# Low parts of two gate blocks on GpSimd instead of VectorE, fewer filter taps there, and weight parts that begin at four different places in their slots

## The chip, the core and the metric

One NeuronCore of a Trainium2 chip runs the whole program. Its engines each work through a queue of their own, strictly in order, and wait for one another by semaphores. The profile's short names are used throughout: PE is TensorE (matrix products), PEld its loads of the stationary operand, DVE is VectorE, ACT is ScalarE, POOL is GpSimd, SP is SyncE, whose queue issues nearly all DMAs. The metric is the device time of one execution in microseconds (us). Before the change the median of three runs is 541.69 us (541.57 to 543.17). One further execution was profiled: 542.99 us, of which 540.7 us lie between its first and last instruction (the span).

## What is computed

One layer of a decoder block on 256 tokens of width 1,024, in float32. What matters here is the first third:

```python
h = rms_norm(x, norm_mix_g)
u, q, kc, vc, ks, vs, kw, vw, g_nsa, g_conv, g_attn = split(h @ w_in)
conv_out = conv_module(u)            # gated, 31-tap filter per channel, layer norm, silu, product
nsa_out  = nsa_attention(q, kc, vc, ks, vs, kw, vw, g_nsa)   # compressed + selected + window attention
y = sigmoid(g_conv) * conv_out + sigmoid(g_attn) * nsa_out
x = x + y @ w_out                    # then cross attention and a SwiGLU FFN
```

`ga0`..`ga3` are the four blocks of `g_attn` (256 channels each), `gc0`..`gc3` those of `g_conv`. The compressed branch first runs a small product over the keys' and values' blocks (`compress_blocks`: sum over 32 positions, then silu).

## The kernel before, in words

**Products in three parts.** PE's fast float32 form (`F32R`) keeps fewer bits, so every operand is held as a high part and a low part, and each product of a GEMM is made three times: high by high, high by low, low by high (`rows`, L234). A block of weights arrives in two halves of 128 partitions x 1,024 elements (512 KB). `raw` (L205) takes one of 4 slots of tag `w` and issues the DMA on SP; `split` (L173) makes the high part on ACT (`hi`, L177) and the low part `lo = w - hi` (L179), on POOL for the names in `aside` (L184: from `u1` to `ga1`) and on DVE for all others. High and low parts have 5 slots each (`whi`, `wlo`), 4,096 bytes long, so they all begin at the same place modulo 4,096. A slot of `w` is free, and the DMA that wants it can leave SP, when both parts of its former tenant are made.

**The filter.** 31 taps per channel, eight blocks of 128 channels, done in pairs. `taps_v` (L411) accumulates on DVE in PSUM (`yp`), one instruction per block and tap (L422). For the first pair, taps 0 to `FIRST_G`-1 = 17 go another way (`taps_g`, L425): ACT multiplies (`vw`, L431), POOL adds into `yt` (L434); DVE does taps 18 to 30 into `part01`, and POOL adds that at the end (L436). `convolve` hands a counted number of such steps to the engines between the GEMMs.

**Gates and first scores.** `gate(0)` and `gate(1)` (L665) multiply `ga0`, `ga1`; between the rows of `gate(1)` stand the compressed scores `cs_ps` (L695), which DVE adds into `nsc` (L698). `gt_ps` (L712) turns the heads' gate logits; ACT takes `sgt` from it (L715), and DVE makes `igc` and `igd` from `sgt` (L718). `scores(0)` (L722) needs two PSUM buffers `s1` (tag `s`, two buffers, one of them last held by `cs_ps`) and one `s0` (tag `s0`, a single buffer, last held by `gt_ps`). Then `between` (L813) goes on with `ga2`, `ga3`, `gc0`..`gc3`, `v0`..`v3`, cut into rows between the attention heads' work.

**What sets the order.** Each engine's queue is laid down when the program is built: a scheduler simulates the engines and takes instructions by priority. `behind(mark)` adds that an instruction comes after `mark` on the same engine. Nothing is reordered at run time: an instruction whose input is late holds up all behind it on its engine, and a DMA that waits on SP holds up all later DMAs.

**The compressed product.** `hidden` (L517) makes `z_ps` in 32 products with 64 columns of weights and 5 x 15 columns of keys or values (rows of 15 out of 16).

Of the kernel before, what the change touches and what calls it, by code (L numbers as in the profile page):

```python
# [10 lines left out]
F32R = mybir.dt.float32r  # L11
AF = mybir.ActivationFunctionType
ALU = mybir.AluOpType
AX = mybir.AxisListType

P = 128
D = 1024
S = 256
NB = D // P
HEADS = 16  # L20
GROUPS = 4
HD = 64
# [8 lines left out]
NCMP = 15  # L31
WARM = 8
LINE = 16
FIRST_G = 18

CHUNKS = (
    [f"k{j}" for j in range(1, 4)] + [f"u{j}" for j in range(8)]
    + ["kc", "vc"] + [f"q{j}" for j in range(4)] + ["ks", "kw", "vs", "vw"]
    + [f"ga{j}" for j in range(4)] + [f"gc{j}" for j in range(4)]
    + [f"pw{j}" for j in range(4)] + [f"wo{j}" for j in range(4)]  # L40
    + [f"xq{j}" for j in range(4)] + [f"v{j}" for j in range(4)]
    + [f"xo{j}" for j in range(4)] + [f"f{j}" for j in range(NF)]
)
CHUNK_AT = {n: i for i, n in enumerate(CHUNKS)}
# [53 lines left out]
def tile_hybrid_block(  # L98
# [49 lines left out]
    def aux(name, shape, tag, bufs):  # L148
        return axp.tile(shape, F32, tag=tag, name=name, bufs=bufs)

    def f(ap):
        return ap.bitcast(F32)
# [18 lines left out]


    def split(w, shape, name):  # L173
        hi = small(f"{name}h", shape, F32R, tag="whi", bufs=5)
        lo = small(f"{name}l", shape, F32R, tag="wlo", bufs=5)
        with behind(*first.get(name, ())):
            copy = nc.scalar.activation(hi, w, AF.Copy)  # L177
            eng = nc.gpsimd if name[:-2] in aside else nc.vector
            splits[name] = copy, eng.tensor_tensor(out=lo, in0=w, in1=f(hi[:]), op=ALU.subtract)  # L179
        return hi, lo  # L180


    first, splits = {}, {}
    aside = CHUNKS[CHUNK_AT["u1"]:CHUNK_AT["ga2"]]  # L184

    def behind(*marks):

# [167 lines left out]
    mem, h = (memh, meml), (hh, hl)  # L355
# [110 lines left out]
    with behind(loads["u6_1"]):  # L466
# [33 lines left out]
    kvt = [long(f"{n}t", slot, (P, 8, GROUPS + 1, 16)) for n, slot in (("k", 11), ("v", 13))]  # L500
    for kv, name in enumerate(("kc", "vc")):
        ps = gemm(name, h)
        kc = kvt[kv]
        for g in range(2):
            for odd in range(2):
                at = ps[HD * g:HD * g + HD].rearrange("p b (m l o) -> p b l m o", l=8, o=2)[:, :, :, :, odd]
# [10 lines left out]
    def hidden():  # L517


        z_ps = aux("z_ps", [P, GROUPS + 1, NCMP], "o", 1)  # L520
        with in_line():
            for l in range(16):
                for kv in range(2):
                    mm = nc.tensor.matmul(z_ps[HD * kv:HD * kv + HD], lhsT=w1t[:, kv, l],
                                          rhs=kvt[kv][:, l % 8, :, l // 8:l // 8 + NCMP], start=l == 0, stop=l == 15)
        last[:] = [mm]
        zs = small("zs", [P, GROUPS, NCMP], tag="zs", bufs=2)
        at = small("at", [P, 1])
        nc.scalar.activation(at, z_ps[:, GROUPS, 0:1], AF.Copy)
        sig = nc.scalar.activation(zs, z_ps[:, :GROUPS], AF.Sigmoid, bias=at)  # L530

        with behind(sig):
            nc.scalar.activation(small("exps", [P, 1]), eps1, AF.Exp)
        z1 = zz[:HD, 0, :64].rearrange("p (g n) -> p g n", g=GROUPS)[:, :, 0:NCMP]
        nc.vector.scalar_tensor_tensor(out=z1, in0=z_ps[:HD, :GROUPS], scalar=at[:HD], in1=zs[:HD], op0=ALU.add, op1=ALU.mult)
        nc.vector.scalar_tensor_tensor(out=zs[HD:], in0=z_ps[HD:, :GROUPS], scalar=at[HD:], in1=zs[HD:], op0=ALU.add, op1=ALU.mult)
        nc.scalar.activation(zz[HD:, 1].rearrange("p (g r n) -> p g r n", g=GROUPS, r=4)[:, :, :, 0:NCMP],
                             zs[HD:].unsqueeze(2).to_broadcast([HD, GROUPS, 4, NCMP]), AF.Copy)

# [17 lines left out]
    for j in range(4):  # L557
# [5 lines left out]
                                       op0=ALU.mult, op1=ALU.subtract)  # L563
        vec = nc.vector.scalar_tensor_tensor(out=q1[0:64], in0=ps[64:128], scalar=-0.125, in1=f(q1[64:128]),
                                             op0=ALU.mult, op1=ALU.subtract)
# [33 lines left out]
    with behind(loads["vw_0"]):  # L599
        nc.sync.dma_start(wg, wgn)  # L600

    wgs = small("wgs", [P, NB, 2, 64], F32R, tag="wlo", bufs=5)
    nc.scalar.activation(wgs[:, :, 0], wg, AF.Copy)
    nc.gpsimd.tensor_tensor(out=wgs[:, :, 1], in0=wg, in1=f(wgs[:, :, 0]), op=ALU.subtract)

# [109 lines left out]
    nc.scalar.activation(sgt, gt_ps, AF.Exp, scale=-1.0)  # L715
    for to, g in ((igc, sgt[:, :, 0:HEADS]), (igd.rearrange("p h t b -> p t b h"),
                                              sgt[:, :, HEADS:3 * HEADS].rearrange("p t (b h) -> p t b h", b=2))):
        nc.vector.tensor_scalar(out=to, in0=g, scalar1=2.0, scalar2=2.0, op0=ALU.mult, op1=ALU.add)  # L718


    def heads_of(hp):
# [2 lines left out]
    def scores(hp):  # L724

        g = hp // 2
        nbp = bias_of(hp)
        s0 = aux(f"s0_{hp}", [P, 2, 2, P], "s0", 1)
        p0 = small(f"p0_{hp}", [P, 2, 2, P], tag="p0", bufs=2)
        p1 = []  # L730
        for k, hd in enumerate(heads_of(hp)):
            s1 = aux(f"s1_{hd}", [P, 2, S], "s", 2)
            with in_line():
                for i, t in enumerate((kdh, kdl)):
                    nc.tensor.matmul(s1, lhsT=qh(hd, 1), rhs=t[:, g].rearrange("p b t -> p (b t)"), start=i == 0, stop=i == 1)  # L735
                for i, t in enumerate((kdh, kdl)):
                    mm = nc.tensor.matmul(s0[:, k], lhsT=qh(hd, 0), rhs=t[:, g, :, 0:P], start=i == 0, stop=i == 1)
            p1.append(small(f"p1_{hd}", [P, 2, S], tag="pr", bufs=4))
            for br in range(2):
                nc.vector.tensor_tensor_reduce(out=p1[k][:, br], in0=s1[:, br], in1=nbp[:, k], scale=1.0, scalar=3e38,  # L740
                                               op0=ALU.add, op1=ALU.min, accum_out=mins[:, hd, 1, br:br + 1])
        last[:] = [mm]
        for k, hd in enumerate(heads_of(hp)):
            for br in range(2):
                least = nc.vector.tensor_tensor_reduce(out=p0[:, k, br], in0=s0[:, k, br], in1=nbp[:, k, P:S], scale=1.0, scalar=3e38,
                                               op0=ALU.add, op1=ALU.min, accum_out=mins[:, hd, 0, br:br + 1])
        first["scores"] = least,
        return p0, p1
# [737 lines left out]
```

## Time and profile before

| what | us |
|---|---|
| median of three runs (541.57 to 543.17) | 541.69 |
| the profiled execution | 542.99 |
| its span | 540.7 |
| PE busy | 529.8 (98%) |
| DVE busy | 455.0 (84%) |
| ACT busy | 357.6 (66%) |
| POOL busy | 155.7 (29%) |

Matmuls are pipelined: each lasts longer than the distance to the next one, so PE counts as busy even where it is slowed. What PE loses shows in two other ways: in rows with an idle time before them, and in the distance between the starts of equal products. Engines other than PE matter where PE, or a DMA that PE's weights come from, waits for them. A timeline row merges equal instructions that follow each other; its columns are start, length, engine, line, operation, output<-inputs, shapes and count.

### The profile page before, as it was taken

The page shows a single profiled execution, that of the slowest core. Times are in us where ns is not written, and L with a number is a line of the kernel's source. Part 1 is how long each engine was busy: PE and PEld are TensorE (multiplying, and loading weights), DVE is VectorE, ACT ScalarE, POOL GpSimd, SP SyncE. Part 2 cuts the span into 40 slices and gives each one's busy share as a digit, 9 for nine tenths or more (in the row PEclk, how much of TensorE's full clock was granted, in tenths as well). Part 3 has the DMA queues.
Part 4 walks back from the last instruction along what each step waited for, and adds up shares of the span by engine and source line. Part 5 has one row for each costly group of instructions (what it writes and reads, how often), then busy time and mean ns, then how long its engine had stood idle before and what let it go on. Part 6 is the DMA issues. An engine that isn't in the chain of part 4 may idle for free.

```text
span 540.7 us, 10518 instructions
## 1 busy us (share of the span) xinstructions
PE 529.8 (98%) x3963; PEld 495.4 (92%) x3963; DVE 455.0 (84%) x913; ACT 357.6 (66%) x649; POOL 155.7 (29%) x109
## 2 busy tenths in 40 slices
PE   9999999999979999999999999999999999999995
PEld 8999999999969988999999999988888888888884
DVE  4868899899989898885869676588899999879996
ACT  4675475787674887969547755576676677648563
POOL 0079999899971000301003100150000000000001
PEclk9999999999979999999999999999999999999999
DMA  8927954665153744438655742757846668438632
GB/s 323 402 83 233 369 180 162 208 195 161 62 183 126 223 151 135 135 98 233 205 198 170 270 138 98 220 171 205 261 158 193 198 208 237 159 121 245 198 118 78
DMA packets 30739, 101.52 MB, mean 188 GB/s; under 512 B 3296, under 2 KB 5856, under 8 KB 30304
## 3 DMA queue, kind: packets, MB, share of 16 engines
q1 hardware_dynamic: 29104, 96.99, 53.8%
q0 software_dynamic: 864, 2.62, 2.8%
q10 hardware_dynamic: 720, 1.23, 0.6%
q8 instruction: 31, 0.51, 0.4%
q14 instruction: 20, 0.16, 0.1%
HBM read 99.59 MB, written 1.25 MB: 186 GB/s over the span
## 4 chain that ended last, share of the span: by engine, by line
PE 60%; DVE 1%; ACT 0%; issue 0%; ACTq 0%; DVEq 0%
PE ps_f L1203 15%; PE ps_f L1205 7%; PE fo L1242 6%; PE ps_xo L246 4%; PE ps_v L246 4%; PE ps_pw L246 4%; PE ps_wo L246 4%; PE ps_xq L246 4%; PE m L1242 4%; PE xo_ps L970 1%; PE xs L970 1%; PE o L801 1%; PE pt_a L780 1%; PE s L735 1%; PE o L798 1%; PE pt_b L780 0%
## 5 line engine op out<-in xcount | busy, mean ns | idle before, releaser
L422 DVE SCALAR_TENSOR_TENSOR yp<-vt,ppt,yp 128x256 f32<-128x256 f32 x196 | 78.4, 486 | 0.2
L1203 PE MATMUL ps_f<-g,f_1h 128*128 128x512 f32 x176 | 49.0, 397 | 0.0
L1203 PE MATMUL ps_f<-g,f_0h 128*128 128x512 f32 x176 | 48.3, 396 | 0.0
L1203 PEld LDWEIGHTS ps_f<-g,f_1h 128*128 128x128 f32 x176 | 32.9, 188 | 7.6
L1203 PEld LDWEIGHTS ps_f<-g,f_0h 128*128 128x128 f32 x176 | 29.9, 188 | 4.0
L179 DVE TENSOR_TENSOR f_1l<-f,f_1h 128x1024 fp32r<-128x1024 f32 x22 | 27.4, 1248 | 5.0 <-ACT f_1h L177 4.1
L1205 PEld LDWEIGHTS ps_f<-g,f_0l 128*128 128x128 f32 x176 | 26.8, 188 | 3.9
L179 DVE TENSOR_TENSOR f_0l<-f,f_0h 128x1024 fp32r<-128x1024 f32 x22 | 26.8, 1219 | 1.8 <-ACT f_0h L177 1.7
L177 ACT ACTIVATE f_1h<-f 128x1024 fp32r<-128x1024 f32 x22 | 23.2, 1056 | 7.0 <-PE ps_xo L246 3.7
L1205 PE MATMUL ps_f<-g,f_0l 128*128 128x256 f32 x176 | 27.4, 277 | 0.0
L179 POOL TENSOR_TENSOR u_0l<-u,u_0h 128x1024 fp32r<-128x1024 f32 x7 | 17.3, 2469 | 31.7 <-ACT u_0h L177 31.7
L434 POOL TENSOR_TENSOR yt<-yt,vw 128x512 f32<-128x512 f32 x17 | 25.2, 1482 | 3.0 <-ACT vw L431 2.7
L1205 PE MATMUL ps_f<-g,f_1l 128*128 128x256 f32 x176 | 25.8, 277 | 0.0
L177 ACT ACTIVATE f_0h<-f 128x1024 fp32r<-128x1024 f32 x22 | 23.1, 1050 | 2.7 <-DMA f<-in_wst_dram 1.3
L1206 ACT ACTIVATE ab<-ps_f 128x256 f32<-128x256 f32 x44 | 16.5, 375 | 11.6 <-PE ps_f L1205 10.9
L755 ACT ACTIVATE p<-p,mins 128x256 f32<-128x256 f32 x32 | 15.9, 503 | 10.3 <-DVE mins L740 10.3
L1205 PEld LDWEIGHTS ps_f<-g,f_1l 128*128 128x128 f32 x176 | 22.6, 188 | 0.0
L1119 POOL DMA_DIRECT2D spare<-in_wfo_dram x1 | 0.9, 866 | 74.2 <-DVE ab L1207 74.2
L1207 DVE TENSOR_TENSOR ab<-ps_f,ab 128x256 f32<-128x256 f32 x44 | 18.3, 419 | 3.0 <-ACT ab L1206 2.8
L290 ACT ACTIVATE uh<-sl 128x256 fp32r<-128x256 f32 x22 | 9.1, 414 | 14.0 <-DVE sl L1211 14.0
L179 POOL TENSOR_TENSOR u_1l<-u,u_1h 128x1024 fp32r<-128x1024 f32 x7 | 17.9, 2552 | 0.0
L310 POOL TENSOR_TENSOR nt_l<-nr_l 128x2 f32<-128x2 f32 x4 | 1.0, 241 | 55.0 <-DVE nr_l L307 54.7
(658 smaller groups left out, 1701.0 us busy)
## 6 DMA issues: line engine op xcount, KB each, us to landing
f<-in_wst_dram SPq DMA_DIRECT2D x44, 512.0 KB, 5.5
fo<-in_wfo_dram SPq DMA_DIRECT2D x16, 512.0 KB, 3.9
u<-in_wst_dram SPq DMA_DIRECT2D x14, 512.0 KB, 8.3
q<-in_wst_dram SPq DMA_DIRECT2D x8, 512.0 KB, 4.5
ga<-in_wst_dram SPq DMA_DIRECT2D x8, 512.0 KB, 4.1
gc<-in_wst_dram SPq DMA_DIRECT2D x8, 512.0 KB, 3.7
v<-in_wst_dram SPq DMA_DIRECT2D x8, 512.0 KB, 6.6
pw<-in_wst_dram SPq DMA_DIRECT2D x8, 512.0 KB, 5.8
```

The lines of the kernel that those rows point to most:

```text
L177: copy = nc.scalar.activation(hi, w, AF.Copy)
L179: splits[name] = copy, eng.tensor_tensor(out=lo, in0=w, in1=f(hi[:]), op=ALU.subtract)
L246: mm = nc.tensor.matmul(ps[:, b], lhsT=lhsT, rhs=rhs, start=row + b + kb == 0, stop=kb == NB - 1 and row == 2 and b == 1)
L422: nc.vector.scalar_tensor_tensor(out=out[:, i] if t == ts[-1] else acc[i], in0=v, scalar=w, in1=acc[i], op0=ALU.mult, op1=ALU.add)
L434: nc.gpsimd.tensor_tensor(out=yt[:, 0:2], in0=yt[:, 0:2], in1=pr, op=ALU.add)
L755: exp.append(nc.scalar.activation(p1[k][:, br], p1[k][:, br], AF.Exp, scale=-1.0, bias=mins[:, hd, 1, br:br + 1], accum_out=sums[:, hd, 1, ...
L970: mm = nc.tensor.matmul(o, lhsT=lhsT, rhs=rhs, start=n == 0, stop=n == len(order) - 1)
L1203: nc.tensor.matmul(ps, lhsT=hs[kb // 4][0][:, kb % 4, cs], rhs=fg[:, :, kb], start=kb == 0, stop=False)
L1205: nc.tensor.matmul(ps[:, 1], lhsT=hs[kb // 4][1][:, kb % 4, cs], rhs=fg[:, 0, kb], start=False, stop=kb == NB - 1)
L1206: nc.scalar.activation(ab[:, b], ps[:, 0], AF.Copy)
L1207: joins[b] = nc.vector.tensor_tensor(out=ab[:, b], in0=ps[:, 1], in1=ab[:, b], op=ALU.add)
L1242: mm = nc.tensor.matmul(o, lhsT=a[x], rhs=b[w], start=start and n == 0, stop=stop and n == 2)
```

## The change

1. `aside` ends at `gc0` instead of `ga2`: the low parts of `ga2` and `ga3` (four halves) are made by POOL instead of DVE.
2. `FIRST_G` is 14 instead of 18: four taps of the first pair go from ACT and POOL (8 multiplications, 4 additions) to DVE (8 instructions of L422).
3. `igc` and `igd` are made by ACT instead of DVE.
4. The halves of `gc0` are set behind the first scores (`first["gc0_0"]`), and after each of its low parts, made by DVE, POOL copies one element of it (`pause_...`), so that POOL's queue waits there for DVE.
5. The slots of high and low parts are 4,160 bytes long, and the parts begin 0, 16, 32 or 48 bytes into them, by turns.
6. `z_ps` takes 65 neighbouring columns instead of 5 x 15.

```diff
-FIRST_G = 18
+SLOT = 1024 + LINE
+FIRST_G = 14
...
     def split(w, shape, name):
-        hi = small(f"{name}h", shape, F32R, tag="whi", bufs=5)
-        lo = small(f"{name}l", shape, F32R, tag="wlo", bufs=5)
+        at = 4 * (len(splits) % 4)
+        hi, lo = (sb.tile([P, SLOT], F32R, tag=f"w{t}", name=f"{name}{t[0]}", bufs=5)[:, at:at + shape[1] * shape[2]].rearrange(
+            "p (k n) -> p k n", k=shape[1]) for t in ("hi", "lo"))
         with behind(*first.get(name, ())):
             copy = nc.scalar.activation(hi, w, AF.Copy)
             eng = nc.gpsimd if name[:-2] in aside else nc.vector
             splits[name] = copy, eng.tensor_tensor(out=lo, in0=w, in1=f(hi[:]), op=ALU.subtract)
+            if name[:-2] == "gc0":
+                nc.gpsimd.tensor_copy(small(f"pause_{name}", [P, 1], tag="exps"), f(lo[:])[:, 0, 0:1])
...
-    aside = CHUNKS[CHUNK_AT["u1"]:CHUNK_AT["ga2"]]
+    aside = CHUNKS[CHUNK_AT["u1"]:CHUNK_AT["gc0"]]
...
-        z_ps = aux("z_ps", [P, GROUPS + 1, NCMP], "o", 1)
+        z_ps = aux("z_ps", [P, 16 * GROUPS + 1], "o", 1)
...
-                                          rhs=kvt[kv][:, l % 8, :, l // 8:l // 8 + NCMP], start=l == 0, stop=l == 15)
+                                          rhs=kvt[kv][:, l % 8].rearrange("p g n -> p (g n)")[:, l // 8:l // 8 + 16 * GROUPS + 1],
+                                          start=l == 0, stop=l == 15)
...
-        nc.vector.tensor_scalar(out=to, in0=g, scalar1=2.0, scalar2=2.0, op0=ALU.mult, op1=ALU.add)
+        nc.scalar.activation(to, g, AF.Copy, scale=2.0, bias=2.0)
...
     p = [scores(0)]
+    first["gc0_0"] = first["scores"]
```

How the queues stand around the first scores. PE's order and the order of the weights' DMAs stay the same there. `ga2_0` is the first half of block `ga2`, an `h` or `l` at its end the high or low part; a last number is the buffer's.

POOL, from the end of `ga1`'s low parts to the sum for the layer norm, before:

```order
L179 TENSOR_TENSOR ga1_1l_2032<-ga1_1_2029,ga1_1h_2031 128x1024
L434 TENSOR_TENSOR yt_354<-yt_354,vw12_1862 128x512
L434 TENSOR_TENSOR yt_354<-yt_354,vw13_1866 128x512
L434 TENSOR_TENSOR yt_354<-yt_354,vw14_1870 128x512
L434 TENSOR_TENSOR yt_354<-yt_354,vw15_1874 128x512
L434 TENSOR_TENSOR yt_354<-yt_354,vw16_1878 128x512
L434 TENSOR_TENSOR yt_354<-yt_354,vw17_1882 128x512
L436 TENSOR_TENSOR yt_354<-yt_354,part01_355 128x512
L626 TENSOR_TENSOR ysum_1915<-yt_354 128x512
```

and with the change:

```order
L181 TENSOR_TENSOR ga1_1l_2024<-ga1_1_2021,ga1_1h_2023 128x1024
L438 TENSOR_TENSOR yt_354<-yt_354,vw12_1870 128x512
L181 TENSOR_TENSOR ga2_0l_2109<-ga2_0_2106,ga2_0h_2108 128x1024
L181 TENSOR_TENSOR ga2_1l_2180<-ga2_1_2177,ga2_1h_2179 128x1024
L181 TENSOR_TENSOR ga3_0l_2212<-ga3_0_2209,ga3_0h_2211 128x1024
L438 TENSOR_TENSOR yt_354<-yt_354,vw13_1874 128x512
L181 TENSOR_TENSOR ga3_1l_2242<-ga3_1_2239,ga3_1h_2241 128x1024
L440 TENSOR_TENSOR yt_354<-yt_354,part01_355 128x512
L183 COPY pause_gc0_0_2304<-gc0_0l_2301 128x1
L633 TENSOR_TENSOR ysum_1907<-yt_354 128x512
```

Four additions are gone, four low parts have come, and two waits for DVE stand around the first addition of the sum.

ACT, from the copies of the keys' low parts (`kdl`) to the first exponentials, before:

```order
L708 ACTIVATE kdl_1538<-kdl_1538 64x2x256 x4
L177 ACTIVATE ga2_1h_2187<-ga2_1_2185 128x1024
L177 ACTIVATE ga3_0h_2219<-ga3_0_2217 128x1024
L662 ACTIVATE sga_1913<-ps_ga0_1916 128x512
L431 ACTIVATE vw16_1878<-vt0_344,ppt_66 128x256 x2
L177 ACTIVATE ga3_1h_2249<-ga3_1_2247 128x1024
L431 ACTIVATE vw17_1882<-vt0_344,ppt_66 128x256 x2
L177 ACTIVATE gc0_0h_2308<-gc0_0_2306 128x1024
L662 ACTIVATE sga_1913<-ps_ga1_1985 128x512
L715 ACTIVATE sgt_2082<-gt_ps_2079 128x96
L755 ACTIVATE p1_0_2098,sums_1982<-p1_0_2098,mins_1984 128x256 x2
```

and with the change:

```order
L715 ACTIVATE kdl_1538<-kdl_1538 64x2x256 x4
L179 ACTIVATE ga2_1h_2179<-ga2_1_2177 128x1024
L179 ACTIVATE ga3_0h_2211<-ga3_0_2209 128x1024
L669 ACTIVATE sga_1905<-ps_ga0_1908 128x512
L179 ACTIVATE ga3_1h_2241<-ga3_1_2239 128x1024
L179 ACTIVATE gc0_0h_2300<-gc0_0_2298 128x1024
L669 ACTIVATE sga_1905<-ps_ga1_1977 128x512
L722 ACTIVATE sgt_2074<-gt_ps_2071 128x96
L725 ACTIVATE igc_1903<-sgt_2074 128x32
L725 ACTIVATE igd_1902<-sgt_2074 128x4x16
```

The multiplications for taps 16 and 17 are gone from between (those for 14 and 15 stood further ahead); `sgt` still stands behind `gc0_0h`.

SP, the DMAs of these weights with what each waits for (DMAHW are semaphores of earlier DMAs, the rest are engines), before:

```order
L210 DMA ga2_0_2114<-in_wst_dram 128x1024 [waits DMAHW7_49,Pool_49]
L210 DMA ga2_1_2185<-in_wst_dram 128x1024 [waits DMAHW0_49,Pool_49]
L210 DMA ga3_0_2217<-in_wst_dram 128x1024 [waits DMAHW5_49,DMAHW3_49,DVE_49]
L210 DMA ga3_1_2247<-in_wst_dram 128x1024 [waits DMAHW1_49,Pool_49]
L210 DMA gc0_0_2306<-in_wst_dram 128x1024 [waits DMAHW2_49,Pool_49]
L210 DMA gc0_1_2336<-in_wst_dram 128x1024 [waits DMAHW4_49,DVE_49]
```

and with the change:

```order
L214 DMA ga2_0_2106<-in_wst_dram 128x1024 [waits DMAHW7_49,Pool_49]
L214 DMA ga2_1_2177<-in_wst_dram 128x1024 [waits DMAHW0_49,Pool_49]
L214 DMA ga3_0_2209<-in_wst_dram 128x1024 [waits DMAHW1_49,DMAHW5_49,Activation_49,Pool_49]
L214 DMA ga3_1_2239<-in_wst_dram 128x1024 [waits DMAHW2_49,Pool_49]
L214 DMA gc0_0_2298<-in_wst_dram 128x1024 [waits DMAHW3_49,Activation_49,Pool_49]
L214 DMA gc0_1_2330<-in_wst_dram 128x1024 [waits DMAHW4_49,Pool_49]
```

The slots of `w` change hands in another order. Before, `ga3_0` takes the slot of `ga2_0` and waits for its low part on DVE, while `ga3_1` and `gc0_0` take those of `ga1_0` and `ga1_1`. With the change `ga3_0` takes the slot of `ga1_0`, `ga3_1` that of `ga1_1`, and `gc0_0` that of `ga2_0`, whose low part POOL makes.

More of the change, by code (lines that the diff above doesn't have):

```diff
@@ L524, in hidden @@
                     mm = nc.tensor.matmul(z_ps[HD * kv:HD * kv + HD], lhsT=w1t[:, kv, l],
-                                          rhs=kvt[kv][:, l % 8, :, l // 8:l // 8 + NCMP], start=l == 0, stop=l == 15)
+                                          rhs=kvt[kv][:, l % 8].rearrange("p g n -> p (g n)")[:, l // 8:l // 8 + 16 * GROUPS + 1],
+                                          start=l == 0, stop=l == 15)
         last[:] = [mm]
+        z_at = z_ps[:, 16 * GROUPS:]
+        z_ps = z_ps[:, 0:16 * GROUPS].rearrange("p (g n) -> p g n", g=GROUPS)[:, :, 0:NCMP]
         zs = small("zs", [P, GROUPS, NCMP], tag="zs", bufs=2)
         at = small("at", [P, 1])
-        nc.scalar.activation(at, z_ps[:, GROUPS, 0:1], AF.Copy)
-        sig = nc.scalar.activation(zs, z_ps[:, :GROUPS], AF.Sigmoid, bias=at)
+        nc.scalar.activation(at, z_at, AF.Copy)
+        sig = nc.scalar.activation(zs, z_ps, AF.Sigmoid, bias=at)
         with behind(sig):
@@ L534, in hidden @@
         z1 = zz[:HD, 0, :64].rearrange("p (g n) -> p g n", g=GROUPS)[:, :, 0:NCMP]
-        nc.vector.scalar_tensor_tensor(out=z1, in0=z_ps[:HD, :GROUPS], scalar=at[:HD], in1=zs[:HD], op0=ALU.add, op1=ALU.mult)
-        nc.vector.scalar_tensor_tensor(out=zs[HD:], in0=z_ps[HD:, :GROUPS], scalar=at[HD:], in1=zs[HD:], op0=ALU.add, op1=ALU.mult)
+        nc.vector.scalar_tensor_tensor(out=z1, in0=z_ps[:HD], scalar=at[:HD], in1=zs[:HD], op0=ALU.add, op1=ALU.mult)
+        nc.vector.scalar_tensor_tensor(out=zs[HD:], in0=z_ps[HD:], scalar=at[HD:], in1=zs[HD:], op0=ALU.add, op1=ALU.mult)
         nc.scalar.activation(zz[HD:, 1].rearrange("p (g r n) -> p g r n", g=GROUPS, r=4)[:, :, :, 0:NCMP],
@@ L600, in tile_hybrid_block @@
         nc.sync.dma_start(wg, wgn)
-    wgs = small("wgs", [P, NB, 2, 64], F32R, tag="wlo", bufs=5)
+    wgs = sb.tile([P, SLOT], F32R, tag="wlo", name="wgs", bufs=5)[:, 0:1024].rearrange("p (k c n) -> p k c n", c=2, n=64)
     nc.scalar.activation(wgs[:, :, 0], wg, AF.Copy)
```

## The prediction

> **What bounds the kernel now.** I read the busy table and the chain of waits first, and then what PE waits for.
>
> ```profile
> PE 529.8 (98%) x3963; PEld 495.4 (92%) x3963; DVE 455.0 (84%) x913; ACT 357.6 (66%) x649; POOL 155.7 (29%) x109
> PE 60%; DVE 1%; ACT 0%; issue 0%; ACTq 0%; DVEq 0%
> PE s L735 <- DVE nsc L698: 2.0, 1, 2.0
> PE s L737 <- ACT sgt L715: 1.8, 1, 1.8
> ```
>
> PE is busy 98% of the span, and the chain runs over PE. The others matter where PE waits for them, and the only two long waits once the first weights are there stand next to each other in `scores(0)`. PE's timeline shows what they cost.
>
> ```profile
> 141.81 1.07 PE L246 MATMUL ps_ga<-hh,ga_0h 128*128 128x256 f32 x8
> 144.47 1.19 PE L246 MATMUL ps_ga<-hh,ga_0l 128*128 128x256 f32 x8
> ...
> 150.45 0.47 PE L735 MATMUL s<-kdh,qt 128*128 128x512 f32 x1
> 150.76 0.40 PE L735 MATMUL s<-kdl,qt 128*128 128x512 f32 x1
> 153.17 0.77 PE L735 MATMUL s<-kdh,qt 128*128 128x512 f32 x1 [2.01 <-DVE nsc L698]
> ...
> 161.11 1.19 PE L246 MATMUL ps_ga<-hh,ga_0l 128*128 128x256 f32 x8
> ...
> 170.61 0.39 PE L735 MATMUL s<-kdh,qt 128*128 128x512 f32 x1
> 171.08 0.28 PE L737 MATMUL s<-kdh,qt 128*128 128x256 f32 x1
> 171.31 0.40 PE L735 MATMUL s<-kdh,qt 128*128 128x512 f32 x1
> 172.00 1.10 PE L246 MATMUL ps_gc<-hh,gc_0h 128*128 128x256 f32 x8
> 153.10:159.90 6.80, 4.95 (x19) 4.26 (x20) 6.76 (x20) 4.88 (x13) 6.56 (x4) 0.50 0.45 155
> ```
>
> From the first score (150.45) to the row of `ga2` at 161.11 pass 10.66 us. Undisturbed, the same work takes 4.1: eight score products as at the next heads (170.61 to 172.00, 1.39) and two rows of a gate with its compressed scores (141.81 to 144.47, 2.66), together 4.05, and 0.08 because the first distance here is 0.31 instead of 0.23. So the place costs 6.5 us: 3.8 in waits, 2.7 because the granted clock (the column before the last two of the last row, a window) is 0.50 for 6.8 us after the first wait.
>
> What is late there starts on DVE.
>
> ```profile
> 138.30 8.05 DVE L179 TENSOR_TENSOR ga_0l<-ga,ga_0h 128x1024 fp32r<-128x1024 f32 x1
> 146.28 5.18 DVE L422 SCALAR_TENSOR_TENSOR yp<-vt,ppt,yp 128x256 f32<-128x256 f32 x13
> 152.15 0.87 DVE L698 TENSOR_TENSOR nsc<-cs_ps,nsc 128x256 f32<-128x256 f32 x2
> 152.94 1.22 DVE L179 TENSOR_TENSOR ga_1l<-ga,ga_1h 128x1024 fp32r<-128x1024 f32 x1
> 137.20 2.46 POOL L179 TENSOR_TENSOR ga_0l<-ga,ga_0h 128x1024 fp32r<-128x1024 f32 x1
> 141.57 2.46 POOL L179 TENSOR_TENSOR ga_1l<-ga,ga_1h 128x1024 fp32r<-128x1024 f32 x1
> 143.92 6.31 POOL L434 TENSOR_TENSOR yt<-yt,vw 128x512 f32<-128x512 f32 x4
> 133.93 1.35 POOL L434 TENSOR_TENSOR yt<-yt,vw 128x512 f32<-128x512 f32 x1
> ```
>
> `ga2_0`'s low part took DVE 8.05 us, where the same operation takes 1.22 a little later; meanwhile POOL ran subtractions, products and additions without a gap. Two things came late by it. DVE reached `nsc`, which frees an `s` buffer, at 152.15 (first wait). And the slot of `ga2_0` came free only at 146.3, so that `ga3_0` landed at 150.4, and ACT, in order, had to work from there without a pause up to `sgt` (second wait):
>
> ```profile
> 150.45 1.06 ACT L177 ACTIVATE ga_0h<-ga 128x1024 fp32r<-128x1024 f32 x1 [6.27 <-DMA ga<-in_wst_dram]
> 153.63 0.90 ACT L431 ACTIVATE vw<-vt,ppt 128x256 f32<-128x256 f32 x2
> 154.43 1.05 ACT L177 ACTIVATE gc_0h<-gc 128x1024 fp32r<-128x1024 f32 x1
> 155.38 0.58 ACT L662 ACTIVATE sga<-ps_ga 128x512 f32<-128x512 f32 x1
> 155.86 0.24 ACT L715 ACTIVATE sgt<-gt_ps 128x96 f32<-128x96 f32 x1
> ga<-in_wst_dram SPq DMA_DIRECT2D x8, 512.0 KB, 4.1
> gc<-in_wst_dram SPq DMA_DIRECT2D x8, 512.0 KB, 3.7
> ```
>
> **The change: low parts, taps and slots of `w`.** DVE loses the 8.05 us operation (138.30 to 146.28 by starts, 7.98) and gains 8 taps at 5.18/13 = 0.40, 3.2 us: if all stood ahead of `nsc`, it starts at 152.15 - 7.98 + 3.2 = 147.4 and is done by 148.3, 2.7 us before PE asks for the buffer at 151.0. The first wait goes. Even with 2.5 us of blocking behind the new POOL work it would stay away.
>
> The second wait shrinks but stays. `ga3_0` and `ga3_1` now follow `ga1`'s low parts on POOL (137.20 + 2.46 = 139.7; 144.0), and land by 4.1 at 143.8 and 148.1. `gc0_0` takes the slot of `ga2_0`, whose low part is POOL's, behind the addition of `vw12`: 144.03 + 1.35 + 2.46 = 147.8. With 3.7 to 4.1 for the transfer it lands at 151.5 to 151.9, and ACT, which has nothing else left ahead of it, needs 0.95 for `gc0_0h`, 0.48 for `sga` (distances of starts, 154.43 to 155.38 to 155.86) and 0.24 for `sgt`: done at 153.2 to 153.6. PE is through with four `s1` products at 151.46 and waits 1.95 us, up to 153.4. Four `s0` products at 0.117 and the 2.66 bring the row of 161.11 to 156.5: **4.6 us saved** at full clock.
>
> Does the clock halve again? In the one row there is, the clock stood at 0.50 from 153.1 on, right behind an idle time of 2.01; that lasted 6.8 us, with a second idle time of 1.79 inside. With one wait left I take half of that length, 3.4 us, in which PE does the work of 1.7: **1.7 us lost**, with both ends kept (0, if it doesn't halve; 2.7 as before). The Trainium skill ("TensorE: Matmul & The Clock Gate", Part 1, "What's actually happening") gives a free-running window of 3,413 ns, of which one idle whole window halves the clock. By it a wait of 1.95 us would cost only itself, and the sum would be 1.7 lower; the trace speaks against it, since the clock fell behind 2.01 us, though 6.8 us is just two such windows.
>
> What stands behind the moved work has time. POOL makes `ga2_1`'s, `ga3_0`'s and `ga3_1`'s low parts up to about 156.5 (three at 2.46, one addition), and PE asks for them from 157 on, later than in sum at half clock. DVE is then free for `gc0_0l`, which PE wants behind 172.00. `pause` makes POOL wait for DVE, and behind it stand only additions for the layer norm. If that cover failed, one low part, 2.46 us, is what PE would wait. The 8 multiplications (0.90/2 = 0.45 each) that ACT loses lie partly in the row before `gc0_0h`; they are in the times above. `igc` and `igd` are two short operations behind `sgt` on either engine.
>
> **`z_ps`.** The view of this line gives its products with their lengths and the first and last start.
>
> ```profile
> L524 PE MATMUL z_ps<-kt,w1t x32: 228/228/279, 97.6 to 99.7; 128*64 128x75 f32 x32
> ```
>
> 32 products with keys, each beside one with values, start within 2.1 us, 65 ns a pair. With 65 columns instead of 75 a pair takes at least 65 x 65/75, 56 ns: 0 to **0.28 us saved**; I take 0.28, since nothing else stands between.
>
> **The slots' new places.** Here the trace has no row of the thing itself; it has rows that say that the place can matter. Equal products come at different distances:
>
> ```profile
> 40.68 1.07 PE L246 MATMUL ps_u<-hh,u_0h 128*128 128x256 f32 x8
> 46.12 1.07 PE L246 MATMUL ps_u<-hh,u_0h 128*128 128x256 f32 x8
> 111.27 1.10 PE L246 MATMUL ps_ks<-hh,ks_0h 128*128 128x256 f32 x8
> 116.92 0.75 PE L246 MATMUL ps_kw<-hh,kw_0h 128*128 128x256 f32 x5
> 326.32 0.64 PE L970 MATMUL xo_ps<-pxl,vxh 128*128 128x256 f32 x4
> 326.79 0.40 PE L246 MATMUL ps_xo<-oxh,xo_0h 128*128 128x256 f32 x2
> 354.00:490.00 136.00, 90.59 (x352) 62.73 (x352) 1.00 0.61 191
> 384.40 1.09 PE L1203 MATMUL ps_f<-g,f_0h 128*128 128x512 f32 x4
> 386.26 0.62 PE L1205 MATMUL ps_f<-g,f_0l 128*128 128x256 f32 x4
> ```
>
> 48 products for `u` take 5.44 us, 113.3 ns each, 48 for `ks` 5.65, 117.7; the four of `xo_ps` 0.47 to 0.48, 120; and eight of 512 columns in the FFN 1.86, 232.5. Nothing waits in these stretches, and the clock is full. In the program's layout the two operands of `xo_ps` begin a multiple of 512 bytes apart, those of `u` and `ks`, as of nearly all others, 64 bytes beside such a multiple: one distance, with a fast and a slow pace. So distance is at most part of it. Measured in this way, from start to start, over all stages, 2,848 products of 256 columns show 1,137 at the slow pace. If the new places make all of them fast, that is 1,137 x 4.4 ns = 5.0 us, and the 352 of the FFN's window (its first row, L1203) at 226.6, twice the fast pace, 2.1 us more: 7.1 less. If they make the 1,711 fast ones slow, it is 7.5 us more. In all these rows the operands begin a multiple of 64 bytes apart; none shows 16, 32 or 48. The layout with the change has 331 products a multiple of 512 apart, 110 more than before, which at 120 ns is up to 0.7 us lost, and spreads the others over all multiples of 16. Nearest are the rows of the most common distance, which have both paces, so I take 0 and keep -7.1 and +7.5. The Trainium skill ("TensorE: Matmul & The Clock Gate", Part 2, "Step-by-step: what each phase is for") gives the streamed operand and the weight loads read ports of their own, so that the one takes nothing from the other. By it no start could change the pace, and the sum would stay as it is; the 113.3 and 117.7 ns of equal products show that something does.
>
> **Sum.** 542.99 - 4.6 - 0.28 + 1.7 = 539.8 for an execution like the profiled one. That one lies 1.3 us above the median of the runs (541.69), so I forecast 539.8 - 1.3 = **538.5 us**.
>
> **Rivals.** (a) The stall goes wholly, because `gc0_0` lands before ACT and PE need it. All of 6.5 + 0.28 off: 541.69 - 6.8 = 534.9. For it: `sgt` hangs on this one transfer; against it: it would have to land 1.95 us earlier, in about half of the 3.7. (b) The new starts quicken the products: 538.5 less up to 7.1, down to 531.4. For it: slow stages exist and nothing waits in them; against it: the layout before has fast and slow at the same distance. (c) **Slower**: the new starts put products now at 113.3 into the pace of `ks`. Place: all stages with a fast pace; price: 4.4 ns a product, up to 538.5 + 7.5 = 546.0. It decides from 543.3 on, when over (543.3 - 538.5)/4.4 ns = 1,090 of the 1,711 have gone slow. For it: the distance of `xo_ps` is always slow, and the new starts go through many distances; against it: only 331 have that one, and those 64 beside it are fast more often than slow. (d) The change doesn't do what it says: POOL, at 2.46 a low part twice as slow as DVE, becomes what is late. If `gc0_0`'s slot comes free one low part later (2.46), 2.1 of the 4.6 us stay, 541.0; with two, nothing stays: 543. For it: four low parts and an addition stand in a row on POOL; against it: the one that counts is the first of them.
>
> **Chances.** Forecast 0.49 (its own range 536.5 to 540.3), (a) 0.08, (b) 0.20, (c) 0.13, (d) 0.10. Runs of one kernel here differ by about 0.3%, 1.6 us, which is what can be told from no change: below 540.1 is faster, above 543.3 slower. Faster: 0.46 of the forecast's, (a), (b), together 0.74; slower: 0.09 of (c) and 0.02 of (d), 0.11; the same: the rest, 0.15. The range that holds 8 in 10 leaves out the lowest of (b), 0.02, and of the others what lies above, about 0.12: **532 to 542**.
>
> **What would show it.** Right: no PE wait for `nsc`; one PE wait for `sgt` of 1.6 to 2.4 us near 151.5; `ga2_0`'s low part on POOL starting near 145.4 and `gc0_0h` on ACT near 151.7; a granted clock of 0.50 for about 3.4 us; from the first score to the third row of `ga2` 7.7 us instead of 10.66. Wrong, by step: a PE wait for `nsc` of any length; a wait for `sgt` over 3 us (case d); `u` or `pw` products of 281 ns instead of 276, or `ks` of 276 (cases c, b). The most doubtful step is the zero for the starts.

## The result, and the profile after

The changed kernel takes 547.83 us (median of four runs, 547.78 to 549.37). The kernel before, in the runs beside it, takes 542.43 (541.57 to 544.16). The ratio is 1.0118, with a 95% interval of 1.0087 to 1.0148: 1.2% slower, where 538.5 us was forecast. The profiled execution took 549.37 us, its span is 547.5, 6.8 more than before. Three single executions fell into a slower state and are left out of the ratios: 546.71 us of the kernel before, 1,478.75 us of the kernel with the new wait taken away, and 884.05 us of the one with 64 floats ahead.

Busy time, chain of waits and PE's waits of the changed kernel:

```profile
PE 536.5 (98%) x3963; PEld 502.3 (92%) x3963; DVE 446.8 (82%) x915; ACT 355.8 (65%) x643; POOL 156.9 (29%) x111
PE 90%; DVE 4%; DMA 4%; ACT 1%; issue 0%; SPq 0%; DVEq 0%; ACTq 0%
PE s L744 <- ACT ptt_b L790: 3.1, 1, 3.1
PE rn L338 <- DVE xtsq L388: 0.7, 1, 0.7
```

Both old waits, for `nsc` and for `sgt`, are gone. A new one of 3.1 us has come, for `ptt_b`, the copy of the first heads' turned weights. PE is busy 6.7 us longer with the same number of instructions, so the products themselves come more slowly. PE's timeline has three places: the products of `u`, the first scores, and the second scores.

```profile
40.57 1.10 PE L250 MATMUL ps_u<-hh,u_1l 128*128 128x256 f32 x8
46.27 1.11 PE L250 MATMUL ps_u<-hh,u_1l 128*128 128x256 f32 x8
...
153.91 0.47 PE L742 MATMUL s<-kdh,qt 128*128 128x512 f32 x1
154.90 0.28 PE L744 MATMUL s<-kdh,qt 128*128 128x256 f32 x1
155.38 1.10 PE L250 MATMUL ps_ga<-hh,ga_0h 128*128 128x256 f32 x8
158.07 1.20 PE L250 MATMUL ps_ga<-hh,ga_0l 128*128 128x256 f32 x8
...
178.17 0.40 PE L742 MATMUL s<-kdl,qt 128*128 128x512 f32 x1
181.70 0.58 PE L744 MATMUL s<-kdh,qt 128*128 128x256 f32 x1 [3.13 <-ACT ptt_b L790]
182.72 1.91 PE L250 MATMUL ps_gc<-hl,gc_0h 128*128 128x256 f32 x8
```

48 products of `u` take 5.70 us, 118.8 ns each, where 113.3 stood before. From the first score to the third row of `ga2` pass 4.16 us (153.91 to 158.07) instead of 10.66; the prediction's undisturbed length was 4.13. Then 3.13 us are lost at the second scores, and in this execution the 3.4 us behind them run at half the clock (0.50 in the third column from the end):

```profile
181.50:184.90 3.40, 3.20 (x15) 3.20 (x16) 2.71 (x17) 3.40 (x16) 0.00 (x0) 0.50 0.55 176
```

The first start of each product, in the two traces, shows where the difference comes from:

| first product of | before, us | after, us | difference |
|---|---|---|---|
| `u` | 28.89 | 29.23 | +0.34 |
| the compressed scores | 142.72 | 146.12 | +3.40 |
| `gc0`, behind the first scores | 172.00 | 169.03 | -2.97 |
| the heads' outputs `o` | 189.42 | 191.62 | +2.20 |
| `xq` (cross attention) | 290.14 | 294.50 | +4.36 |
| the FFN | 354.41 | 359.10 | +4.69 |
| `end`, the last group | 531.94 | 538.44 | +6.51 |

PE loses 3.1 us gradually from `u` to the first scores, gains 6.4 there, loses 5.2 at the second scores, and loses again gradually to the end. Three effects are mixed, then: the old stall went, a new one came, and the pace fell. The half clock belongs to the profiled execution alone: 3.4 us at half clock take 0.003 off the mean granted clock, which is 0.996 there, while the three other executions have 0.998 or 0.999 and take 547.8 us.

Why the old stall went is in the timelines of DVE, POOL and ACT:

```profile
150.86 0.88 DVE L705 TENSOR_TENSOR nsc<-cs_ps,nsc 128x256 f32<-128x256 f32 x2 [2.15 <-PE cs_ps L702]
146.04 2.38 POOL L181 TENSOR_TENSOR ga_0l<-ga,ga_0h 128x1024 fp32r<-128x1024 f32 x1
152.29 1.06 ACT L179 ACTIVATE gc_0h<-gc 128x1024 fp32r<-128x1024 f32 x1 [2.39 <-DMA gc<-in_wst_dram]
154.13 0.25 ACT L722 ACTIVATE sgt<-gt_ps 128x96 f32<-128x96 f32 x1 [0.23 <-PE gt_ps L719]
```

DVE now waits for PE at `nsc`. ACT waits for PE at `sgt`; PE itself comes 3.4 us later. Why the new one came is in ACT's and SP's:

```profile
174.94 0.59 ACT L790 ACTIVATE ptt_a<-pt_a 128x512 f32<-128x512 f32 x1
179.62 1.06 ACT L179 ACTIVATE gc_0h<-gc 128x1024 fp32r<-128x1024 f32 x1 [4.08 <-DMA gc<-in_wst_dram]
180.58 0.58 ACT L790 ACTIVATE ptt_a<-pt_a 128x512 f32<-128x512 f32 x1
181.06 0.59 ACT L790 ACTIVATE ptt_b<-pt_b 128x512 f32<-128x512 f32 x1
...
172.66 1.26 SPq L214 DMA_DIRECT2D gc<-in_wst_dram  x2
174.72 7.62 SPq L214 DMA_DIRECT2D v<-in_wst_dram  x3
```

The copy `gc3_0h` stands between the first heads' copies and waits for its DMA, issued at 172.66; `ptt_b`, which frees PE's `s0` buffer, stands behind it. In the kernel before, ACT's queue has another order there. This is the scheduler's doing, and the order of the two programs shows it (before, then after; `gc_0h<-gc_0_...` is `gc3_0h`):

```
L783 ACTIVATE ptt_a_2370<-pt_a_2365 128x512
L783 ACTIVATE ptt_a_2377<-pt_a_2372 128x512
L783 ACTIVATE ptt_b_2384<-pt_b_2379 128x512

L790 ACTIVATE ptt_a_2366<-pt_a_2361 128x512
L179 ACTIVATE gc_0h<-gc_0_2704 128x1024
L790 ACTIVATE ptt_a_2373<-pt_a_2368 128x512
L790 ACTIVATE ptt_b_2380<-pt_b_2375 128x512
```

### The profile page after: what moved, and what is told of

The parts are those of the page before. It is cut to its first block, busy times and chain, and to the rows that moved or that the text cites. A ratio compares the mean times of both kernels' runs of the same rounds, so it can differ in the third digit from the quotient of the medians.

```text
span 547.5 us, 10516 instructions
## 1 busy us (share of the span) xinstructions
PE 536.5 (98%) x3963; PEld 502.3 (92%) x3963; DVE 446.8 (82%) x915; ACT 355.8 (65%) x643; POOL 156.9 (29%) x111
## 4 chain that ended last, share of the span: by engine, by line
PE 90%; DVE 4%; DMA 4%; ACT 1%; issue 0%; SPq 0%; DVEq 0%; ACTq 0%
PE ps_f L1211 15%; PE ps_u L250 8%; PE ps_f L1213 8%; PE fo L1250 6%; PE ps_pw L250 4%; PE ps_q L250 4%; PE ps_xq L250 4%; PE ps_wo L250 4%; PE ps_v L250 4%; PE ps_xo L250 4%; PE m L1250 4%; PE ps_gc L250 3%; PE ps_ga L250 2%; PE ps_k L250 2%; DMA xtsq<-in_xt_dram 2%; PE o L808 1%
## 5 line engine op out<-in xcount | busy, mean ns | idle before, releaser
L426 DVE SCALAR_TENSOR_TENSOR yp<-vt,ppt,yp 128x256 f32<-128x256 f32 x204 | 81.6, 481 | 0.2
L438 POOL TENSOR_TENSOR yt<-yt,vw 128x512 f32<-128x512 f32 x13 | 16.8, 1292 | 0.0
```

Of the source, the lines that this page charges most:

```text
L426: nc.vector.scalar_tensor_tensor(out=out[:, i] if t == ts[-1] else acc[i], in0=v, scalar=w, in1=acc[i], op0=ALU.mult, op1=ALU.add)
L438: nc.gpsimd.tensor_tensor(out=yt[:, 0:2], in0=yt[:, 0:2], in1=pr, op=ALU.add)
```

## The experiments

All medians are of the experiment's own runs. The kernel before, beside them on the same chips, had medians of 541.97 to 542.54, and single runs between 537.7 and 545.2.

Of an execution that wasn't profiled, the time and the mean granted clock are known. In the kernel before they go together: of 78 executions, 11 have a mean clock of 0.998 or 0.999, which leaves no room for 3.4 us at half clock, and take 537.7 to 541.8 us; 27 have 0.992, as the profiled one has with its 6.8 us at half clock, and take 541.9 to 544.0; 7 have 0.988 and take 543.3 to 545.2. So the half clock behind the old stall isn't there in every execution, and part of a gain over the median of 542.5 is that it is gone.

**The slots taken back.** The change with the old slots of 4,096 bytes.

```diff
-        at = 4 * (len(splits) % 4)
-        hi, lo = (sb.tile([P, SLOT], F32R, tag=f"w{t}", ...)[:, at:at + ...] ...)
+        hi = small(f"{name}h", shape, F32R, tag="whi", bufs=5)
+        lo = small(f"{name}l", shape, F32R, tag="wlo", bufs=5)
```

> The change, but the high and low parts in slots of 4,096 bytes that begin as before. Theory (the new starts put nearly all products of 256 columns at 118 ns; the four low parts on POOL end the old stall, but a new order on ACT, gc3_0's high part ahead of ptt_b, makes a new one of 3.1 us): the pace goes back, about 1,140 slow products of 2,840 instead of 2,460, 8 us less; PE then comes to the first scores 3.4 us earlier and waits 2 to 2.6 us for sgt, and the wait for ptt_b stays: 541.5 to 543.5 us. Rival (the starts are harmless, and the slow pace comes from what the other engines now do at other times): 547.8 us, pace as with the change.

542.57 us, ratio 1.0007 (0.9981 to 1.0032): as expected, and 5.3 us under the change. The wait for `ptt_b` stays:

```profile
PE s L743 <- ACT ptt_b L789: 3.3, 1, 3.3
```

A wait for `sgt` doesn't come; that part of the expectation is a miss. The pace came back only in part: 51% of the products of 256 columns come at 113 to 114 ns, where the kernel before has 60%. The view of PE's lines over the stage of `u` has

```profile
L249 PE MATMUL ps_u<-hl,u_0h x63: 281/281/281, 29.8 to 71.0; 128*128 128x256 f32 x63
```

281 ns is the length of each product there. The kernel before has 276 in the same view:

```profile
L246 PE MATMUL ps_u<-hl,u_0h x64: 276/276/276, 29.8 to 69.6; 128*128 128x256 f32 x64
```

The slow pace exists with the old starts too.

**The slots alone.** The kernel before with the new slots and nothing else of the change.

```diff
-        hi = small(f"{name}h", shape, F32R, tag="whi", bufs=5)
-        lo = small(f"{name}l", shape, F32R, tag="wlo", bufs=5)
+        at = 4 * (len(splits) % 4)
+        hi, lo = (sb.tile([P, SLOT], F32R, tag=f"w{t}", ...)[:, at:at + ...] ...)
```

> The kernel before, with only the slots of 4,160 bytes and the starts 0, 16, 32, 48 bytes into them. Theory: 8 us lost in the pace, part of it given back, because PE comes 3.4 us later to the first scores and finds nsc ready and sgt nearly so (about 4 us less there): 545 to 547.5 us; no wait for ptt_b, since ACT's order there is that of before. Rival (starts harmless): 541.7 us.

548.87 us, ratio 1.0126 (1.0056 to 1.0195). The rival falls: the starts alone cost 6.3 us, with DVE's, ACT's and POOL's work of before. It is 1.4 more than the theory's upper end. In the profiled execution the clock halved for 6.8 us behind the one wait that is left, for `sgt` (1.78 us), and the other executions fit that: three of the four have a mean clock of 0.991 to 0.994, and the one with 0.998 took 547.23 us, inside the theory's range.

```profile
158.10:164.80 6.70, 6.70 (x34) 6.70 (x33) 6.58 (x22) 4.57 (x17) 6.32 (x5) 0.50 0.42 139
```

**The new wait taken away.** The change, with `gc3_0`'s parts behind the copy `ptt_b`, as they stand before.

```diff
         tb = turned(f"b{hp}", [p1[k][:, br, P:S] for k in range(2) for br in range(2)])
         if hp == 0:
+            first["gc3_0"] = copies[-1],
```

> The change, and gc3_0's high part set behind the copy ptt_b on ACT, as it stands in the kernel before. Theory: the wait of 3.13 us and the half clock behind it go, 3.1 to 5 us less: 543 to 544.7 us; pace as slow as with the change. Rival (PE would wait for gc3_0's weights themselves soon after, since their DMA lands late): the time stays within 1 us of 547.8 and the wait moves to a row of gc3.

543.98 us, 3.85 under the change, and PE has no wait left in the whole program but the one before its first product:

```profile
PE warm L355 <- DVE eps_t L161: 1.1, 1, 1.1
```

The rival falls: no wait for `gc3`'s weights took its place.

**Both.** Old slots, and `gc3_0`'s parts behind `ptt_b`.

> Both: slots as before and gc3_0's high part behind ptt_b. Theory: 541.7 less 6.5 for the old stall, plus a wait of 2 to 2.6 us for sgt and perhaps half a clock window (1.7): 537 to 539.5 us. Rival (each of the two is only part of what slows the change): 541 to 545 us.

536.53 us, ratio 0.9912 (0.9878 to 0.9945): 1.1% faster than before, and 7.45 us faster than the kernel with the same orders and the new starts. Taken back in this order, 7.45 us is the price of the starts, 3.85 that of the new order, and 6.0 what the rest of the change gains over the median of before. Taken back the other way round the prices differ: 5.26 for the starts while the new wait is there (547.83 less 542.57), and 6.04 for the new order with the old starts (542.57 less 536.53). The half clock behind that wait is part of the difference: nine of the ten executions with the old slots and the wait have a mean clock of 0.991 to 0.995, and the three unprofiled ones of the changed kernel have 0.998 or 0.999. Both effects are there in either order; their sizes are known to about 2 us.

Lines of the kernel with both: `u` by lines, the wait that is left, and the clock behind it.

```profile
L249 PE MATMUL ps_u<-hl,u_0h x64: 276/276/276, 30.0 to 69.7; 128*128 128x256 f32 x64
...
149.35 0.47 PE L741 MATMUL s<-kdh,qt 128*128 128x512 f32 x1
151.81 0.39 PE L743 MATMUL s<-kdh,qt 128*128 128x256 f32 x1 [1.28 <-ACT sgt L721]
155.06 1.19 PE L249 MATMUL ps_ga<-hh,ga_0l 128*128 128x256 f32 x8
...
153.00:156.50 3.50, 3.50 (x33) 3.50 (x32) 3.50 (x7) 3.50 (x15) 2.94 (x2) 1.00 0.53 178
```

All of `u` is at 276 ns here and was at 281 in the run with old slots above, though all queues hold the same instructions in the same order, at the same addresses, until long after `u` (the first difference is `gc3_0h`, past 170 us). Which pace a stage has at these starts is decided in the execution, then, and not by the program alone.

**Which starts.** Five kernels put the parts elsewhere. The first three have `gc3_0`'s parts behind `ptt_b`, and so compare with 536.53 and 543.98 us. In the first, 16 bytes more stand ahead of all old slots; since buffers are rounded up to 32 bytes, the operands came to lie 96 and 416 bytes apart modulo 512, not 80 as the text below says:

```diff
-        return nc.scalar.activation(small(name, [P, 1]), eps_t[:, 0:1], AF.Sqrt)
+        return nc.scalar.activation(sb.tile([P, LINE + 4], F32, tag=name, name=name, bufs=1)[:, 0:1], eps_t[:, 0:1], AF.Sqrt)
```

> Slots of 4,096 bytes and gc3_0's part behind ptt_b, as in the kernel of 536.5 us, but 16 bytes stand ahead of all slots, so that nearly every product has its operands 80 or 432 instead of 64 or 448 bytes apart modulo 512 (32 and 96 in some views of the layout). Theory A (a distance that stays the same from product to product is enough for the pace of 113 ns): 536 to 538 us. Theory B (only certain distances, multiples of 64, allow it): pace 118, 543 to 545 us.

545.23 us. A constant distance isn't enough: theory A falls. 48 products of `u` take 5.76 us here, 120.0 ns each:

```profile
40.55 1.12 PE L249 MATMUL ps_u<-hh,u_1l 128*128 128x256 f32 x8
46.31 0.88 PE L249 MATMUL ps_u<-hh,u_1l 128*128 128x256 f32 x6
```

The second has 16 floats there instead of 4, which makes 128.

> The same with 64 bytes ahead of the slots: nearly all products 128 bytes beside a multiple of 512. Theory A (a constant distance is enough): 536 to 538 us. Theory B (odd multiples of 64 alone allow the fast pace, as the groups of the changed kernel's trace by distance hint: 64, 192 and 320 have products at 113 ns, 128 and 256 next to none): 543 to 545 us.

545.83 us: no better. Lines of these two in the stage of `u`, the first kernel's, then the second's:

```profile
L249 PE MATMUL ps_u<-hl,u_0h x64: 282/283/283, 30.0 to 72.1; 128*128 128x256 f32 x64
```

```profile
L249 PE MATMUL ps_u<-hl,u_0h x63: 279/281/285, 29.8 to 71.3; 128*128 128x256 f32 x63
```

The third has the change's longer slots but no starts inside them, so that distances run through all multiples of 64.

```diff
-        at = 4 * (len(splits) % 4)
+        at = 0
```

> The change with gc3_0's part behind ptt_b, slots of 4,160 bytes, but all parts begin at the slot's start: distances are multiples of 64 that change from slot to slot. Theory A (constant distance): pace 118 nearly everywhere, 543 to 545 us, as with the four starts. Theory B (odd multiples of 64): about half of the products can be fast, 539 to 542 us. Theory C (only the 16, 32 and 48 bytes hurt): 536 to 538 us.

541.83 us, ratio 0.9999 (0.9978 to 1.0019): between the two, as theory B has it. Grouped by distance (from the program's layout), its products of 256 columns come at 113 to 114 ns in 44, 42, 65 and 27% of the cases at 64, 192, 320 and 448 bytes, and in 6, 7, 3 and 6% at 0, 128, 256 and 384.

Two last kernels test the other odd multiples, with 32 and with 64 floats ahead of the slots, and `gc0_0h` behind `sgt` (the next experiment).

> Slots as before, gc3_0's part behind ptt_b, gc0_0's behind sgt, and 128 bytes ahead of all slots: nearly all products 192 bytes beside a multiple of 512. Theory B (odd multiples of 64 allow the pace of 113 ns): 535.5 to 537.5 us, two thirds of the 256-column products at 113. Rival (only 64 beside a multiple of 512 does): 544 to 546 us.

539.09 us, 1.6 above what was expected, and 2.9 above the same kernel at 64 bytes (536.15); the share at 113 to 114 ns is 26%, not two thirds.

> The same with 256 bytes ahead of the slots: 320 (the other side: 192) bytes beside a multiple of 512. Theory B: 535.5 to 537.5 us; since in the kernel with drifting starts the products at 320 were at 113 more often (65%) than those at 64 and 192 (about 43%), it may be up to 2 us less. Rival (only 64): 544 to 546 us.

536.49 us over three executions (535.50 to 537.49; 536.99 with the fourth), as expected, but not under the 536.15 of the kernel at 64 bytes. Together:

| kernel | distance modulo 512 | of the 256-column products at 113 to 114 ns | us |
|---|---|---|---|
| before | 64, 448 | 60% | 542.43 |
| old slots, both orders mended | 64, 448 | 69% | 536.15 |
| 64 floats ahead | 320, 192 | 54% | 536.49 |
| 32 floats ahead | 192, 320 | 26% | 539.09 |
| slots of 4,160, no starts | all multiples of 64 | 27% | 541.83 |
| 16 floats ahead | 128, 384 | 2% | 545.83 |
| 4 floats ahead | 96, 416 | 0.3% | 545.23 |
| the change's slots, alone | all multiples of 16 | 8% | 548.87 |
| the change | all multiples of 16 | 8% | 547.83 |

The shares are of one execution each, from start to start, over some 2,800 products. The times of the kernel before, of the slots alone and of the change hold long waits as well, those of the others none over 0.6 us. Where the operands begin an odd multiple of 64 bytes apart, a product can come every 113.3 ns, and can also come every 117.8. At 96 and 128 bytes it practically never reaches 113.3; in the kernels with spread starts a few small groups at other multiples of 16 reach it in up to about a fifth of the cases.

One reading is left open by all nine. In their layouts one operand of every product of 256 columns begins at a multiple of 512 bytes, so the distance is at the same time the place where the other operand itself begins. Whether the distance or that place decides can't be told apart here. What in the chip makes this so, and what decides between the two paces within one program, these runs don't show.

**The last wait.** Old slots, `gc3_0`'s parts behind `ptt_b`, and `gc0_0h` behind `sgt` on ACT.

```diff
-    nc.scalar.activation(sgt, gt_ps, AF.Exp, scale=-1.0)
+    gates = nc.scalar.activation(sgt, gt_ps, AF.Exp, scale=-1.0)
-    first["gc0_0"] = first["scores"]
+    first["gc0_0"] = gates, *first["scores"]
```

> Slots as before, gc3_0's part behind ptt_b, and gc0_0's high part behind sgt on ACT. The wait of 1.28 us for sgt that the kernel of 536.5 us has left should go: 535 to 535.5 us. Rival: gc0_0's parts come late for something else (igc, igd and the exponentials stand behind it): 536.5 us or more.

536.15 us, ratio 0.9912 (0.9881 to 0.9943). The wait for `sgt` is gone, but only 0.4 of its 1.28 us shows in the median, less than expected; `f_1h` is now waited for (0.5 us) later. The two medians can't be told apart. Both kernels beat the one before and the changed one.

**Which part of the change ended the old stall.** First the low parts of `ga2` and `ga3` back on DVE, in the kernel of 536.53 us.

```diff
-    aside = CHUNKS[CHUNK_AT["u1"]:CHUNK_AT["gc0"]]
+    aside = CHUNKS[CHUNK_AT["u1"]:CHUNK_AT["ga2"]]
```

> The kernel of 536.5 us (slots as before, gc3_0's part behind ptt_b), with the low parts of ga2 and ga3 back on DVE. Theory (what ends the old stall is that ga2_0's low part and nsc no longer stand behind a blocked DVE): DVE's low part of ga2_0 is held up by POOL's work again, though POOL has four additions less behind ga1's low parts, so the wait for sgt grows from 1.3 to 3 us or more: 538 to 541 us. Rival (fewer taps on ACT and POOL are what did it): 536 to 537 us.

542.62 us: all 6.1 us are lost again, 1.6 more than the theory's upper end. Nine of the ten executions take 541.2 to 543.6 us at a mean clock of 0.991 to 0.993; the tenth takes 537.57 at 0.999, so this loss too isn't there in every execution. In the profiled one PE waits for `nsc`, not for `sgt`:

```profile
155.62 0.77 PE L741 MATMUL s<-kdh,qt 128*128 128x512 f32 x1 [6.09 <-DVE nsc L704]
...
137.45 8.23 DVE L180 TENSOR_TENSOR ga_0l<-ga,ga_0h 128x1024 fp32r<-128x1024 f32 x1
145.60 8.31 DVE L425 SCALAR_TENSOR_TENSOR yp<-vt,ppt,yp 128x256 f32<-128x256 f32 x21
136.62 2.40 POOL L180 TENSOR_TENSOR ga_0l<-ga,ga_0h 128x1024 fp32r<-128x1024 f32 x1
138.97 2.05 POOL L685 TENSOR_TENSOR vcm<-vcs,cpt 128x512 fp32r<-128x512 f32 x2
140.99 2.37 POOL L180 TENSOR_TENSOR ga_1l<-ga,ga_1h 128x1024 fp32r<-128x1024 f32 x1
143.32 3.51 POOL L437 TENSOR_TENSOR yt<-yt,vw 128x512 f32<-128x512 f32 x2
```

The long subtraction on DVE is back with 8.23 us beside POOL's unbroken work, and now all eight taps moved to DVE stand ahead of `nsc` as well. Then the taps, with the low parts left on POOL:

```diff
-FIRST_G = 14
+FIRST_G = 18
```

> The same kernel with 18 instead of 14 taps of the first pair on ACT and POOL, the low parts of ga2 and ga3 still on POOL. Theory: ACT has one pair of multiplications (0.9 us) more ahead of gc0_0's part, and POOL's additions stand behind the low parts that count, so the wait for sgt grows by at most 1 us: 536.5 to 538 us. Rival (the room made by 14 taps is needed): 540 us or more.

539.33 us, between the theory's 538 and the rival's 540. In the profiled execution (540.97 us) the wait for `sgt` is 2.66 us instead of 1.28, and the clock halves behind it for 3.4 us:

```profile
153.46 0.38 PE L743 MATMUL s<-kdh,qt 128*128 128x256 f32 x1 [2.66 <-ACT sgt L721]
...
153.20:156.60 3.40, 3.14 (x17) 3.14 (x17) 2.30 (x9) 3.37 (x16) 3.40 (x3) 0.62 0.55 176
```

So the room is worth 2.8 us, and the low parts on POOL are what ends the stall. The two don't add up, since either taken back alone shows what it costs while the other stands: 6.1 and 2.8 us against 6.0 for all. `igc` and `igd` on ACT and the narrower `z_ps` were not tried apart.

## Why the prediction was wrong, by its steps

- **"I take 0" for the slots' new places** is the step that failed most. It put at nothing what costs 7.45 us without the new wait (5.3 to 6.3 us in the other comparisons). That is at the end of the range kept for it (+7.5), and rival (c), given 0.13, is what came: of its 1,711 fast products, counted there as those under 115.5 ns, 1,349 are gone (362 of 2,823 are left), where it was to decide from 1,090. The rows of the most common distance have both paces, and from this I concluded that distance was at most part of it and took the middle. The right reading was that 64 and 448 are among the few distances that have a fast pace at all. The row that pointed there was quoted: `xo_ps`, whose 48 products, at a multiple of 512, come every 119.7 ns on the mean. A spread over all multiples of 16 leaves the good distances, whatever the reason. The price per product was low as well: the changed kernel's products come every 118.0 ns on the mean, those still at 113 included, and not every 117.7.
- **The rule of two read ports** (the Trainium skill, "TensorE: Matmul & The Clock Gate", Part 2, "Step-by-step: what each phase is for") says that loading weights takes no read bandwidth from the running product. The prediction drew from it that no start could change the pace, which is more than the rule says, and the runs refute that: 543.98 and 536.53 us differ in starts alone. Whether the ports have to do with it, no run shows.
- **"What stands behind the moved work has time"** failed as well. It looked at POOL's and DVE's parts, and at ACT's order only up to the first exponentials. The scheduler had also moved `gc3_0h` ahead of `ptt_b`, some 15 rows further on. The wait cost 3.85 us in the median, and in the profiled execution the half clock behind it came on top. No rival had it.
- **Low parts and taps: right in the mechanism.** The first wait went, with DVE early at `nsc`. The second shrank and stayed when the pace was good: 1.28 us where 1.95 was worked out. `gc0_0h` began at 150.07 instead of near 151.7, while PE came only 1.1 us earlier to the first scores (149.35 for 150.45). From first score to third row of `ga2` pass 5.71 us (149.35 to 155.06) instead of 10.66: 4.95 saved for 4.6 forecast. In the changed kernel it went wholly, as in rival (a), but there PE came 3.4 us later, which isn't a gain.
- **1.7 us for a half clock** was not needed behind the wait of 1.28. Behind longer waits a half clock of 3.4 us, the length assumed, came in some executions and not in others, as the mean clocks show; in the changed kernel it came in one of four, behind the new wait. The size was right; whether it comes is a matter for the range, not for the sum.
- **`z_ps`** saved 0.21 us (from its first product to the next `q` product 2.23 us before, 2.02 after) for 0.28.
- **The sum, beside the forecast:** without the new starts and the new order the change takes 536.53 us, 2.0 under the forecast of 538.5; the 1.7 for the clock is the largest part of that. The two steps that were put at nothing add 3.85 (new order) and 7.45 (starts): 547.83. These steps are differences of the medians themselves, so that they add up proves nothing. The 6.0 us gained over the kernel before hold the old stall, `z_ps`, and a pace that was better at the same starts: 70% of the products at 113 to 114 ns in the profiled execution, for 60%.

## What to carry to other kernels

When a change moves operands in SBUF, compare the distance of starts of equal products, not only waits: a few ns on each of thousands of products weigh as much as a stall, and no view of waits shows them. When a scheduler sets the order, compare the queue of the engine that PE waits for to the end, not only around the edit. And a change that bundles a gain with a neutral-looking edit should be timed apart: here 1.1% faster became 1.2% slower by the two.

## What the runs showed of the hardware that was not expected

- A product of 128x128 by 256 columns in F32R can come every 113.3 ns where its two operands begin an odd multiple of 64 bytes apart, one of them at a multiple of 512, and hardly elsewhere; at 96 bytes it comes every 120.0 over the whole of `u` and at 128 every 118.7, without any wait in these stretches.
- With the same instructions and addresses the stage of `u` was wholly at 113.3 ns in one execution and wholly at 117.8 in another. The kernel before spreads over 7.5 us (537.7 to 545.2), which goes with its mean clock; the kernel with the new starts and no waits stayed within 1.2 us in nine executions (543.6 to 544.8), at 0.996 to 0.999.
- In the profiled executions a single PE wait of 1.28 us left the clock at full speed, and behind single waits of 1.78, 2.66, 3.13, 3.3 and 6.09 us it was halved, for 3.4 or 6.8 us. The length of the wait alone doesn't decide, as far as the mean clocks show: three of the changed kernel's four executions had no room for such a stretch. The Trainium skill ("TensorE: Matmul & The Clock Gate", Part 1, "What's actually happening") asks for an idle window of about 3.4 us; here a wait of 1.78 us, about half of that, was enough, while the lengths of 3.4 and 6.8 us fit one and two of its windows.
- A DVE subtraction with two SBUF operands took 8.05 and 8.23 us beside POOL's unbroken work, through five POOL operations in a row, and 1.22 on the mean of 22 in the FFN, where POOL does next to nothing. The Trainium skill ("SBUF — State Buffer", "Who interferes with whom") says that such a DVE instruction contends with a GpSimd instruction that reads SBUF, and that the contention is an exclusive lock. The 8 us agree with it.
